# Placing side work behind sparse steps in the instruction order of a two-branch encoder kernel

## The chip, the cores and the metric

The kernel runs on one core of one Trainium2 chip. The metric is device time in microseconds (us) of one execution. The program is built by a tile framework: every instruction is traced in Python, the order of TensorE (PE) is kept as traced, and the order of the other engines (VectorE = DVE, ScalarE = ACT, GpSimd = POOL, and SyncE = SP, which issues nearly all DMAs) is chosen by a scheduler when the program is built, from its own estimate of when each instruction becomes ready. Among ready instructions the one traced first goes first. Once built, each engine's order is fixed.

## What is computed

Two sequences (1 x 1024 and 1 x 2048 tokens of width 1024) go through one encoder layer, each with the same 16 meta tokens ahead of it:

```
xn   = rmsnorm(h, g_pre);  proj = xn @ w_in + b_in          # 1024 -> 6672 columns
ya   = neighbourhood_attention(q, k, v) * silu(z)  @ w_a     # 8 heads of 64, 8 x 16 windows
yb   = mlstm_both_directions(conv(qk), v, gates) * silu(z) @ w_b   # 4 heads of 128
y    = (sigmoid(ga) * ya + sigmoid(gb) * yb) @ w_out
out  = h + rmsnorm(y, g_post)                                # meta tokens dropped
```

All of it is float32. The kernel reaches that by splitting every operand of a large product into a rounded high part and a low remainder and adding three products.

## The kernel before, in words

**Two streams on one TensorE.** `run` (L2070) interleaves two generators. `dense` does the projections and the output products; each of its yields stands for about 1.4 us of matmuls. `sparse` does, in the order of `STEPS`, the mLSTM of the short sequence, its attention, the mLSTM of the long sequence and its attention. Each of its yields ends a *sparse step* and gives a weight; `run` then advances `dense` until it has issued as much. So the traced order is: the instructions of one sparse step, then a dense chunk or two, then the next sparse step. Within the mLSTM a step holds, for example, `conv_c` (L1608 to L1612: the query q is finished and split), and the next but few hold `scores` (L1658), the matmul that reads q. Within the attention a unit's scores (L1210), exponential (L1225), scaling (L1235), transposes and their split (L1244, L1249) and output product (L1257) lie in steps that follow each other.

**Groups of dense work.** `PLAN` lists groups (sequence, first token of 1024, columns). The first is the short sequence's mLSTM columns, the second its attention columns, the third the first 1024 tokens of the long sequence with both kinds, the fourth the next 1024 tokens. A group (`group`, L1011) goes through jobs of four feature-major columns, each for two halves of 512 tokens, and token-major units. After each column a half is *evacuated* from PSUM (`fm_evac`: L682, L688 to L694 and a store).

**x's build.** `build_half` (L466) makes one half of the normalised input: it loads four token tiles (`tokens`, L398), squares them on ACT (L355), computes reciprocal roots on DVE (`rsqrt8`, L161 to L166), makes diagonals (L367, L369), spreads them over rows with a matmul (L375), loads the transposed input (`xt`, L405), scales it on DVE (L523), and splits it on ACT (L530) and DVE (L531). For the long sequence this happens four times. The tiles all come from four buffers called `xr`. The build is a generator; `spread` (L881) advances it a little at every dense yield: 12/15 of a piece per yield while the first part runs beside the last job of the group before (up to "scaled"), 22/15 otherwise.

**Side work.** Products of gate and attention columns are done later with Strassen-Winograd's seven products instead of eight. Their sums are made beforehand: `wprep` (L563) makes the sums of eight pairs of weight columns (raw tile `pr`, split to `po`: L567, L580, L589), 13 pieces a pair; `tprep` (L624) makes those of x (L627, L659, stores L663), 36 pieces for the short sequence; `nprep` (L597) those of six more pairs. `beside` (L545) is called once per dense yield and counts a turn; a piece of a side runs in every turn that its step divides. At the start of the first attention what is left of the weight sum is drained, in the last job of the second group what is left of x's sum.

**What holds a piece back.** `behind` (L189) puts every instruction traced inside it, by an ordering edge without a semaphore, behind the last marked instruction of its own engine. `mark` (L182) marks, for DVE, ACT and SP, the last instruction from a given position on:

```
for x in self.nc.cur_bb.bb.instructions[start:]:
    if x.engine in (DVE, Activation, SP):
        self.marks[x.engine] = x
```

Before the change only evacuations (`fm_evac`, `tm_unit`) mark. Pieces of the sides, the stores of kept x and the loads of the sums (`tload`, L909) are traced under `behind`; pieces of x's build are not.

Of the kernel before, what the change touches and what calls it, by code (L numbers as in the profile page):

```python
# [57 lines left out]
def _weight_units():  # L58

    return ([("i", x, P) for x in FM_COLS] + [("t", *c, a) for c in TM_COLS for a in range(2)]  # L60
            + [("m", f, P) for f in range(KT)] + [("o", c, a) for c in range(4) for a in range(2)])
# [76 lines left out]
class K:  # L138
# [327 lines left out]
    def build_half(self, s, t0, res):  # L466

        nc, wp = self.nc, self.wp
        if (s, t0) in self.xkept:
            assert not self.xput  # L470
            yield
            yield "scaled"
            x = []
            for name, part in zip(("xh", "xl"), self.xkept[s, t0]):
                x.append(wp.tile([P, KT, HALF], F32R, name=name, bufs=2))
                for k in range(0, KT, 4):
                    nc.sync.dma_start(x[-1][:, k:k + 4, :512].bitcast(F32), part[:, k:k + 4, :])
                yield
            res.append(tuple(x))
            return  # L480
        if s == 0:
            xts = self.xnext
            self.xnext = None
            while self.rwait:
                yield "wait"
            self.early = False
            yield "scaled"
            g = self.gpre
            p = self.psum("sm", [P, 512])
            nc.tensor.matmul(p[:, :KT], self.ident, g, start=True, stop=True)  # L490
            g = self.cp.tile([P, KT], F32, name="gx")
            nc.vector.tensor_copy(g, p[:, :KT])
            x, r = self.xparts(), []
            for e in range(4):
                self.xsplit(x, xts[e], e, 0, g)
                self.wflush(2)
                yield
            res.append(tuple(x))
            yield from self.rsum(self.toks, r)
            nc.vector.tensor_copy(self.rc[:, 4:8], r[0])  # L500
            dg = self.rdiag(r[0], self.toks[0][0])

            def rows():
                self.rrows(dg, self.rr[:, 1], "sm")
                self.xp.close()
                self.wside = self.wprep()
                self.sides.append([self.wside, 3])
            self.rwait[s, t0] = rows
        else:
            bp = self.bp  # L510
            toks, r = self.tokens(s, t0, range(4), bp, 4), []
            yield
            yield from self.rsum(toks, r)
            dg = self.rdiag(r[0], toks[3][0])
            xts = [self.xtload(s, t0, e, bp, 4) for e in range(3)]
            yield
            rr = bp.tile([P, 512], F32, name="rx", tag="thT", bufs=1)
            self.rrows(dg, rr, "pj")
            xts.append(self.xtload(s, t0, 3, bp, 4))
            yield  # L520
            for k in range(KT):
                v = xts[k // 2][:, k % 2]
                nc.vector.scalar_tensor_tensor(v, v, self.gpre[:, k:k + 1], rr, op0=ALU.mult, op1=ALU.mult)  # L523
                if k % 2:
                    yield
            yield "scaled"
            x = self.xparts()
            for e in range(4):
                h = x[0][:, 2 * e:2 * e + 2, :512]
                nc.scalar.activation(h, xts[e], AF.Copy)  # L530
                nc.vector.tensor_tensor(x[1][:, 2 * e:2 * e + 2, :512], xts[e], h.bitcast(F32), op=ALU.subtract)  # L531
                yield
            res.append(tuple(x))
            self.xkeep(s, t0, x)
# [28 lines left out]
    def wprep(self):  # L563

        nc = self.nc
        unit = {k: j for j, k in enumerate(_weight_units())}
        sub = lambda o, a, b: nc.vector.tensor_tensor(o, a, b, op=ALU.subtract)  # L567
        self.pq = ExitStack()
        pool = self.pq.enter_context(self.tc.tile_pool(name="pq", bufs=1, side="right", reuse_waits="tile"))
        for p in range(6, 14):  # L570
            if p == 12:
                [x for x in self.sides if x[0] is self.wside][0][1] = 6
            raw = pool.tile([P, 2, 2, 512], F32, name="pr", bufs=1)
            for f in range(2):
                nc.sync.dma_start(raw[:, f].rearrange("p a c -> p (a c)"), self.i["wu"][unit["i", PAIRS[p][f], P], :, :D])
            for _ in range(3):
                yield
            for f, ops in ((0, ("11", "12")), (1, ("21", "22")), (1, ("s3", "s1")), (0, ("s2", "s4"))):
                if ops[0] == "s3":
                    nc.vector.tensor_tensor(raw[:, 1, 1], raw[:, 1, 0], raw[:, 1, 1], op=ALU.add)  # L580
                    sub(raw[:, 1, 0], raw[:, 0, 0], raw[:, 1, 0])
                    yield
                if ops[0] == "s2":
                    sub(raw[:, 0, 0], raw[:, 1, 1], raw[:, 0, 0])
                    sub(raw[:, 0, 1], raw[:, 0, 1], raw[:, 0, 0])
                    yield
                o = pool.tile([P, 2, 2, 512], F32R, name="po", bufs=1)
                c = slice(p > 7 and ops[0] == "21", 2)
                nc.scalar.activation(o[:, c, 0], raw[:, f, c], AF.Copy)  # L589
                sub(o[:, c, 1], raw[:, f, c], o[:, c, 0].bitcast(F32))  # L590
                for q, op in list(enumerate(ops))[c]:
                    d = self.qd[p, op] = self.dp.tile([P, D], F32, name=f"q{p}{op}")
                    nc.sync.dma_start(d[:, :], o[:, q].rearrange("p a c -> p (a c)").bitcast(F32))
                yield
                yield
# [285 lines left out]
    def spread(self, gen, chunks, until=None):  # L881

        steps = 22 if until is None else 12

        def side(last=False):
            nonlocal acc, over
            acc += steps / chunks
            while not over and (acc >= 1.0 or last):
                acc -= 1.0
                x = next(gen, "end")  # L890
                over = x == "end" or (until is not None and x == until)
                if x == "wait":
                    break
        acc, over = 0.0, False
        return side
# [115 lines left out]
    def group(self, s, t0, meta, cols, reuse, nxt):  # L1011
# [4 lines left out]
        sw = (s, t0) in SW  # L1016
        if sw and not reuse:
            self.tside = chain(self.tprep(s, t0, 34 if s == 0 else 370 if t0 == 0 else 0), self.nprep() if t0 else ())
            self.sides.append([self.tside, 6 if s == 0 else 2 if t0 else 3])
        for j, (kind, c) in enumerate(jobs):  # L1020
            if kind == "tm":
                for cost in self.tm_unit(c[0], [(x,) + h for x, h in zip(self.xs, todo)], c[1]):
# [1047 lines left out]
    def run(self, ctx):  # L2070
        self.done = set()
        self.setup(ctx)
        dense, acc = self.dense(ctx), 0.0
        for w in self.sparse():
            if isinstance(w, tuple):
                while w not in self.done:
                    assert next(dense) is not True
                continue
            acc += w
            while acc > 0.0:  # L2080
                d = next(dense, None)
                if d is None or d is True:
                    acc = 0.0
                    break
                acc -= d
        for w in dense:
            assert w is not True

# [60 lines left out]
```

## Time and profile before

| | us |
|---|---|
| median of 3 runs | 2712.49 (2710.47 to 2716.36) |
| profiled execution | 2712.26 |
| its span in the trace | 2710.5 |
| PE busy | 2645.7 |
| DVE busy | 1937.3 |
| ACT busy | 1440.0 |
| mean granted clock of PE | 0.992 |

The profile gives each engine's busy time, groups of instructions by line, who waited for whom, the chain of work that ended last, and a timeline. L12 is line 12 of the kernel. "`A <- B`" behind a wait means that the engine of A stood idle until B was done. A granted clock below 1 means that TensorE was throttled in part of that stretch. Busy times of PE are modelled from matmuls that overlap; what counts here is PE's idle time.

### The profile page before, as it was taken

The numbers are of one execution on the slowest core, as the hardware profiler recorded it, in microseconds if no ns is written. First come the engines' busy times: TensorE is split into PE (matmuls) and PEld (weight loads), VectorE is DVE, ScalarE is ACT, GpSimd is POOL, SyncE is SP. The second block draws the span as 40 slices with busy tenths as digits, with TensorE's granted clock in tenths as the row PEclk, the third lists the DMA queues.
The fourth block names the chain that finished last, engine by engine and source line by source line (L and its number), as shares of the span: only waits on it lengthen the run. The fifth ranks groups of instructions, "written<-read, shape, count | busy, mean of one in ns | idle before, by whom it ended". The sixth has DMA issues, their size and how long they took to land.

```text
span 2710.5 us, 47460 instructions
## 1 busy us (share of the span) xinstructions
PE 2645.7 (98%) x15928; PEld 2334.1 (86%) x15928; DVE 1937.3 (71%) x5266; ACT 1440.0 (53%) x3388; POOL 16.9 (1%) x100
## 2 busy tenths in 40 slices
PE   9999998999998999999999999999999999999998
PEld 7998787889977899878888888888778998989888
DVE  5655787869847888536766767757368889897954
ACT  5323565665345655446655566556365656656521
POOL 0000000000000000000000000000000000000000
PEclk9999998999999999999999999999999999999999
DMA  9888898899896899798888998899899799998965
GB/s 363 342 321 317 295 340 297 306 338 314 280 322 210 307 329 310 239 311 266 265 283 293 368 311 263 281 323 378 259 300 298 246 311 274 293 294 280 329 230 203
DMA packets 411652, 805.75 MB, mean 297 GB/s; under 512 B 52016, under 2 KB 180992, under 8 KB 409104
## 3 DMA queue, kind: packets, MB, share of 16 engines
q1 hardware_dynamic: 410288, 800.04, 88.4%
q0 software_dynamic: 1120, 2.69, 0.4%
q8 instruction: 126, 2.06, 0.3%
q14 instruction: 118, 0.97, 0.1%
HBM read 548.96 MB, written 253.60 MB: 296 GB/s over the span
## 4 chain that ended last, share of the span: by engine, by line
PE 84%; DMA 6%; DVE 6%; ACT 2%; issue 1%; SPq 1%; DVEq 0%; ACTq 0%
PE pj L202 9%; PE pj L203 9%; PE pj L204 9%; PE pj L963 7%; PE pj L965 7%; PE pj L964 7%; PE pj L772 4%; PE pj L774 4%; PE pj L773 4%; PE pj L1908 3%; PE pj L1910 3%; PE pj L1909 3%; PE sm L1257 2%; PE tr L1242 2%; DMA xt<-xt 1%
## 5 line engine op out<-in xcount | busy, mean ns | idle before, releaser
L202 PE MATMUL pj<-xh,whi 128*128 128x512 f32 (+1 forms) x896 | 346.3, 387 | 2.0 <-ACT whi L303 2.0
L203 PE MATMUL pj<-xl,whi 128*128 128x512 f32 (+1 forms) x896 | 337.9, 377 | 0.1
L204 PE MATMUL pj<-xh,wlo 128*128 128x512 f32 (+1 forms) x896 | 337.6, 377 | 0.3 <-DVE wlo L304 0.3
L772 PE MATMUL pj<-whi,xh 128*128 128x256 f32 (+1 forms) x1152 | 330.1, 287 | 0.0
L773 PE MATMUL pj<-wlo,xh 128*128 128x256 f32 (+1 forms) x1152 | 325.1, 282 | 0.0
L774 PE MATMUL pj<-whi,xl 128*128 128x256 f32 (+1 forms) x1152 | 324.9, 282 | 0.0
L1908 PE MATMUL pj<-whi,mh 128*128 128x256 f32 x768 | 219.5, 286 | 0.7 <-DMA whi<-wh 0.7
L772 PEld LDWEIGHTS pj<-whi,xh 128*128 128x128 f32 x1152 | 217.4, 189 | 0.2
L773 PEld LDWEIGHTS pj<-wlo,xh 128*128 128x128 f32 x1152 | 217.4, 189 | 0.1
L774 PEld LDWEIGHTS pj<-whi,xl 128*128 128x128 f32 x1152 | 217.2, 189 | 0.0
L1910 PE MATMUL pj<-whi,mlo 128*128 128x256 f32 x768 | 216.4, 282 | 0.0
L1909 PE MATMUL pj<-wlo,mh 128*128 128x256 f32 x768 | 216.3, 282 | 0.0
L204 PEld LDWEIGHTS pj<-xh,wlo 128*128 128x128 f32 x896 | 170.4, 190 | 33.2 <-DVE wlo L304 0.5
L202 PEld LDWEIGHTS pj<-xh,whi 128*128 128x128 f32 x896 | 170.8, 191 | 30.4 <-ACT whi L303 2.9
L203 PEld LDWEIGHTS pj<-xl,whi 128*128 128x128 f32 x896 | 170.8, 191 | 26.7 <-issue 1.0
L202 PE MATMUL pj<-yh,whi 128*128 128x512 f32 x384 | 154.6, 402 | 0.0
L203 PE MATMUL pj<-yl,whi 128*128 128x512 f32 x384 | 151.2, 394 | 0.7 <-DVE yl L1810 0.7
L204 PE MATMUL pj<-yh,wlo 128*128 128x512 f32 x384 | 151.6, 395 | 0.0
L1244 ACT ACTIVATE pts<-tr 96x384 fp32r<-96x384 f32 (+2 forms) x192 | 103.2, 538 | 86.9 <-PE tr L1242 86.4
L1908 PEld LDWEIGHTS pj<-whi,mh 128*128 128x128 f32 x768 | 145.1, 189 | 1.7 <-DMA whi<-wh 0.9
L1909 PEld LDWEIGHTS pj<-wlo,mh 128*128 128x128 f32 x768 | 145.1, 189 | 0.8
L1910 PEld LDWEIGHTS pj<-whi,mlo 128*128 128x128 f32 x768 | 145.1, 189 | 0.0
(366 smaller groups left out, 6940.5 us busy)
## 6 DMA issues: line engine op xcount, KB each, us to landing
whi<-wh SPq DMA_DIRECT2D x136, 512.0 KB
wlo<-wl SPq DMA_DIRECT2D x136, 512.0 KB
whi<-q SPq DMA_DIRECT2D x62, 512.0 KB
wlo<-q SPq DMA_DIRECT2D x50, 512.0 KB
wraw<-wu SPq DMA_DIRECT2D x48, 512.0 KB
gt<-st SPq DMA_DIRECT2D x96, 256.0 KB
tg<-gt SPq DMA_DIRECT2D x96, 256.0 KB
wh<-whi SPq DMA_DIRECT2D x36, 512.0 KB
```

Of the source, the lines that this page charges most:

```text
L202: mm(out, ah, bh, start=start, stop=False)
L203: mm(out, ah, bl, start=False, stop=False)
L204: mm(out, al, bh, start=False, stop=stop)
L772: nc.tensor.matmul(o, xh, wh, start=k == 0, stop=False)
L773: nc.tensor.matmul(o, xh, wl, start=False, stop=False)
L774: nc.tensor.matmul(o, xl, wh, start=False, stop=k == KT - 1)
L963: mm(bank, w[:, 0, k], xh[:, k], start=fresh and k == 0, stop=False, skip_group_check=True)
L964: mm(bank, w[:, 0, k], xl[:, k], start=False, stop=False, skip_group_check=True)
L965: mm(bank, w[:, 1, k], xh[:, k], start=False, stop=k == 3, skip_group_check=True)
L1908: nc.tensor.matmul(o, mh[:, k, xs], wh, start=clear > 0 and k == 0, stop=False)
L1909: nc.tensor.matmul(o, mh[:, k, xs], wl, start=False, stop=False)
L1910: nc.tensor.matmul(o, ml[:, k, xs], wh, start=False, stop=clear < 2 and k == KT - 1)
```

## The change

There are four edits. `run` now takes the sparse generator step by step, notes where the instruction list stood, and marks the instructions of each sparse step, so that whatever is traced under `behind` next stands behind the last DVE, ACT and SP instruction of the latest sparse step or evacuation, whichever was traced later. `spread` advances x's build under `behind`. The weight sum runs in every fourth turn (before: every third, and from its seventh pair on every sixth). The short sequence's x sum runs in every fourth turn (before: every sixth).

```diff
@@ build_half
-                self.sides.append([self.wside, 3])
+                self.sides.append([self.wside, 4])
@@ wprep
         for p in range(6, 14):
-            if p == 12:
-                [x for x in self.sides if x[0] is self.wside][0][1] = 6
             raw = pool.tile([P, 2, 2, 512], F32, name="pr", bufs=1)
@@ spread
             while not over and (acc >= 1.0 or last):
                 acc -= 1.0
-                x = next(gen, "end")
+                with self.behind():
+                    x = next(gen, "end")
@@ group
-            self.sides.append([self.tside, 6 if s == 0 else 2 if t0 else 3])
+            self.sides.append([self.tside, 4 if s == 0 else 2 if t0 else 3])
@@ run
-        for w in self.sparse():
+        sparse, start = self.sparse(), 0
+        while (w := next(sparse, None)) is not None:
+            self.mark(start)
             if isinstance(w, tuple):
                 while w not in self.done:
                     assert next(dense) is not True
+                start = len(self.nc.cur_bb.bb.instructions)
                 continue
             acc += w
             while acc > 0.0:
...
                 acc -= d
+            start = len(self.nc.cur_bb.bb.instructions)
```

## The prediction

> **What bounds the kernel now.** I read the page's busy lines first, then the stage table (columns: stretch, length, busy time of PE, PEld, DVE, ACT, POOL with instruction counts, granted clock, DMA share, GB/s), then who PE waited for.
>
> ```profile
> span 2710.5 us, 47460 instructions
> PE 2645.7 (98%) x15928; PEld 2334.1 (86%) x15928; DVE 1937.3 (71%) x5266; ACT 1440.0 (53%) x3388; POOL 16.9 (1%) x100
> ```
>
> ```profile
> 0.00:250.00 250.00, 246.56 (x1619) 223.92 (x1620) 142.45 (x243) 102.18 (x153) 1.71 (x25) 1.00 0.90 335
> 250.00:420.00 170.00, 160.68 (x1037) 143.93 (x1036) 133.07 (x366) 92.64 (x215) 3.61 (x17) 0.97 0.90 319
> 420.00:600.00 180.00, 167.37 (x826) 138.64 (x825) 135.78 (x367) 107.34 (x258) 1.01 (x8) 0.96 0.91 313
> 600.00:745.00 145.00, 143.36 (x1206) 142.93 (x1204) 127.53 (x377) 67.69 (x170) 2.67 (x10) 1.00 0.90 302
> 745.00:960.00 215.00, 204.40 (x1108) 173.69 (x1107) 152.32 (x354) 122.02 (x244) 0.51 (x1) 0.98 0.85 278
> ```
>
> TensorE (PE) is the bound, and the edit changes no matmul. What can change is PE's idle time: 2710.5 − 2645.7 = 64.8 us, of which 9.3 + 12.6 + 1.6 + 10.6 = 34.1 us lie between 250 and 960 us, where x's build and the side work run beside sparse steps. Beyond 960 us only the loads of `tload` are touched. So the prize is about 34 us, and the clock that goes with it. PE's waits from 0 to 900 us (us in total, times, longest) say where it lies:
>
> ```profile
> PE sc L1658 <- DVE q L1612: 12.4, 2, 11.0
> PE tr L1789 <- DVE hb L1784: 3.2, 1, 3.2
> PE sc L1210 <- ACT prb L1225: 3.0, 1, 3.0
> PE sm L1257 <- DVE pts L1249: 2.8, 1, 2.8
> PE sm L1210 <- DVE yg L1272: 2.3, 1, 2.3
> PE sm L203 <- DVE vwl L1510: 2.0, 1, 2.0
> PE sm L1379 <- DVE g_eT L1381: 1.8, 1, 1.8
> ```
>
> Each is a sparse step's instruction that came late on DVE or ACT. The timelines up to the end of the longest, DVE, then ACT (start, length, what):
>
> ```profile
> 451.98 1.21 DVE L531 TENSOR_TENSOR xl<-xt,xh 128x1024 fp32r<-128x1024 f32 x1
> ...
> 453.38 3.49 DVE L531 TENSOR_TENSOR xl<-xt,xh 128x1024 fp32r<-128x1024 f32 x3
> ...
> 457.65 1.21 DVE L567 TENSOR_TENSOR po<-pr,po 128x1024 fp32r<-128x1024 f32 x1
> 458.79 0.41 DVE L1612 TENSOR_TENSOR q<-cv,q 128x256 fp32r<-128x256 f32 x1
> ```
> ```profile
> 448.37 0.42 ACT L1421 ACTIVATE th<-cv 128x256 f32<-128x256 f32 x1
> ...
> 449.20 3.88 ACT L530 ACTIVATE xh<-xt 128x1024 fp32r<-128x1024 f32 x4
> ...
> 454.12 1.05 ACT L589 ACTIVATE po<-pr 128x1024 fp32r<-128x1024 f32 x1
> 455.07 0.41 ACT L1611 ACTIVATE q<-cv 128x256 fp32r<-128x256 f32 x1
> ```
>
> In the program's order `conv_c` (L1608 to L1612) comes one sparse step ahead of the scores (L1658) at which PE stands. The four L530/L531 are issued only in the second half of the last job, after those scores. The scheduler let them overtake: 3.88 us on ACT and 1.21 + 3.49 us on DVE, and 1.05 and 1.21 us of a weight sum, ran ahead of L1611 and L1612. This is what the edit forbids.
>
> **The change part by part.** I count turns (calls of `beside`, one per dense yield). The first group has 24 half columns of 4 and 68 of its token-major units, 164; the second 132, to turn 296; the third 192, to 488. The rr matmul L375 is the eighth piece of a build, so at 0.8 a turn from turn 264 the first one of x_sample falls at turn 274, and at 1.47 a turn from 488 the last at 494:
>
> ```profile
> L375 PE MATMUL pj<-xr,ones x8: 590/591/592, 436.8 to 817.1; 128*128 128x512 f32 x8
> ```
>
> (817.1 − 436.8) / 220 = 1.73 us a turn.
>
> *Build behind the sparse step.* (a) At 448 us (459.2 − 11.0): L1421 ends at 448.8; with L530, L531 and the weight sum behind the scores, L1608 (no longer than its neighbours) and L1611 and L1612 (0.41 us each) and up to three evacuation pieces end near 452 instead of 459.2. Gain 7 us of 11.0 (bounds 0 and 11.0).
>
> ```profile
> 790.83 1.06 ACT L355 ACTIVATE xsq<-xr 128x1024 bf16<-128x1024 f32 x1 [0.88 <-DMA xr<-x_sample]
> ```
> ```profile
> 785.29 5.52 DMA xr<-x_sample
> ```
> ```profile
> 828.49 1.41 DVE L523 SCALAR_TENSOR_TENSOR xt<-xt,gpre,rx 128x512 f32<-128x512 f32 x2 [2.78 <-DMA xt<-xt]
> ```
>
> (b) PE's wait on prb: the square L355 waits for its load and stands ahead of the exponential L1225 that PE wants, though it is issued at turn 489 or 490, 4 turns (7 us) before the L375 at 817, so near 810. Pinned there it can't block: 2.5 of 3.0 us. (c) PE's waits on pts and yg: L531 and a sum (L627) run among the attention steps there: half of 2.8 + 2.3, so 2.5 us; the wait of 2.78 us for xt stays.
>
> *Step of x's sum, 6 to 4.* It starts at turn 36 and has 36 pieces: the last falls at turn 176 instead of 246. After turn 164 (about 250 us) 3 pieces are left instead of 14. Its DVE time from 250 to 420 us, and then that of the weight sum (what touches `pr`) in three stages:
>
> ```profile
> 250.00:420.00 170.00, 17.70 (x20) 0.97 0.90 319
> ```
> ```profile
> 250.00:420.00 170.00, 17.96 (x20) 9.64 (x10) 0.97 0.90 319
> 420.00:600.00 180.00, 8.30 (x9) 4.83 (x5) 0.96 0.91 313
> 600.00:745.00 145.00, 5.83 (x7) 2.72 (x3) 1.00 0.90 302
> ```
>
> So 11/14 × 17.7 = 13.9 us of DVE move ahead of 250 us, where DVE is 57% busy and PE idles 3.4 us, most of it the opening; I cost them at nothing there (bounds 0 and 8 us, since the slower weight sum takes 11 pieces, 5.8 us, out). They also free x's four `xr` buffers 70 turns earlier; the loads into these hold the squares on ACT now:
>
> ```profile
> 395.89 1.06 ACT L355 ACTIVATE xsq<-xr 128x1024 bf16<-128x1024 f32 x1 [4.04 <-DMA xr<-x_sample]
> ```
>
> (d) ACT's late work feeds PE's wait of 3.2 us for L1784: gain 2.5. (e) The waits on vwl and g_eT and what is left of L1658's (2.0 + 1.8 + 12.4 − 11.0 = 5.2 us) lie in that stage, where 8 of 34 weight pieces (4 us) go too and DVE falls from 78% to (133.1 − 17.9) / 170 = 68%: half, 2.6 (bounds 0 and 5.2).
>
> *Step of the weight sum, 3 and 6 to 4.* 104 pieces from turn 32 end at turn 444 instead of 416, just before the first mLSTM's end (about 453), so nothing is drained in a lump. Today 34 of them fall from turn 165 to 268, about the stage from 250 to 420 us: 17.96 / 34 = 0.53 us of DVE a piece. From 268 to 365 turns there are 8 more (4.2 us, DVE at 135.8 / 180 = 75%: 0.5 us charged), from 365 to 453 there are 11 more, 6 us where DVE is 127.5 / 145 = 88% busy: I charge 1.5 us (bounds 0 and 6).
>
> *What is queued.* A load that is pinned stands behind the sparse step's last SP issue, and its reader stands one or two pieces behind it. A square comes one piece after its load: 0.8 pieces a turn in a last job, 1.47 in a first, so 2.2 or 1.2 us later, and the load takes 5.5 us. ACT would hold 3.3 + 4.3 us for the two kinds, twice each: 15.2 us, with exponentials and evacuations behind it. Today's holds:
>
> ```profile
> ACT xsq L355 <- DMA xr<-x_sample: 36.5, 12, 21.2
> ```
>
> PE paid about 6.2 us (the 3.2 and the 3.0) for 36.5. At that rate 15.2 us cost 2.6; all of it would be 15.2. Nearer the former: 4 us. For `xt` (L405 to L523) I take today's holds as unchanged. The loads of `tload` and the stores of kept x go behind the same SP issues; several turns lie before their data is read, so 0 (bounds 0 and 3.0, PE's longest wait on ACT in the list). POOL is never marked.
>
> **Clock.** Stalls lower the granted clock:
>
> ```profile
> 450.00:500.00 50.00, 40.74 (x187) 33.66 (x187) 41.86 (x107) 36.34 (x85) 0.30 (x3) 0.86 0.92 326
> 800.00:850.00 50.00, 44.42 (x214) 35.83 (x213) 36.39 (x92) 27.31 (x57) 0.00 (x0) 0.97 0.59 179
> ```
>
> 0.14 × 50 = 7 us of full clock are missing around the longest stall, 1.5 us around 800. I take 3 us back (bounds 0 and 7). The Trainium skill (TensorE: Matmul & The Clock Gate, What's actually happening) has TensorE fall to half rate after an idle window of about 3.4 us. The stretch from 800 to 850 us, with the waits of 2.8 and 2.3 us, shows 0.97 all the same, so the measurement doesn't support that length as a floor; by the rule a stall cut from 11 to 4 us would still cost the clock, and the sum would lose those 3 us.
>
> **Sum.** −(7 + 2.5 + 2.5 + 2.5 + 2.6) − 3 + 0.5 + 1.5 + 4 = −14.1 us. The profiled execution took 2712.26 us, its span 2710.5, and the median shown is 2712.49: forecast **2698 us**.
>
> **The rivals.**
> *Slower: x's loads lose their lead.* One mechanism, in the four builds of x_sample: pinned loads land after their readers stand at the head of ACT and DVE. For it: L355 and L523 wait today already, and this load took longer than any gap here:
>
> ```profile
> 817.70 10.76 DMA xt<-xt
> ```
> ```profile
> DVE xt L523 <- DMA xt<-xt: 8.3, 3, 4.7
> ```
>
> L523 comes two pieces after its load, 4.3 or 2.4 us; holds are then up to 6.5 and 8.4 us, 29.8 us for four builds against 8.3 now. If PE pays the 15.2 us whole in place of 6.2 (9 more), half of the added 21.5, and 2 us for the fuller DVE, and only (a) with half the clock comes back (8.5), the time is 13 us longer: 2725 us. It decides from the point where PE pays two fifths of that (8.5 of 21.7). Against it: the row above holds a single wait of 21.2 us, and no wait of PE on ACT in the list is over 3.0 us. The Trainium skill (Perfetto Trace Analysis, Tensor Engine Instruction) calls ACT and DVE strict FIFO; the rows at 790.83 and 828.49 agree.
> *The wait only moves.* (a) shrinks, (c) and (e) come, with half the clock, but the displaced L530/L531 and the holds (9) and the fuller DVE (2) eat them: −7 − 2.5 − 2.6 − 1.5 + 9 + 2 = −2.6, 2710 us.
> *It doesn't do what it says.* The side work already stands behind evacuations; if the order written hardly differs, only the steps act, (d) and (e) less the weight sum's charges: 2712 − 5.1 + 2 = 2709 us. The overtaking rows speak against it.
>
> **How the numbers follow.** Forecast and its neighbours, −6 to −34 us (all waits (a) to (e) gone and the clock back: 27.5 + 7): 0.58, own range 2682 to 2706. The two unmoved cases: 0.09 and 0.06. Slower: 0.27. A measurement here can't tell less than 0.2% (5.4 us) from no change. The range runs from 2682 to 2728: below it lies 0.06 (nearly all terms at their bound), above it a little under half of the slower case, 0.12.
>
> **What would show it.** Right: around 448 us no L530/L531 between L1608 and L1612, and a wait at L1658 under 5 us; the last product of x's sum with `rr` (piece 29, turn 148) ahead of 250 us; the weight sum's end (turn 444) near 437 + 170 × 1.73 = 731 us; idle time from 250 to 960 us down to about 20 us. Wrong: L355 and L523 holding ACT and DVE for over 4 us each with PE waiting on L1225, L1249 or L1612 behind them; new waits from 600 to 745 us.

## The result and the profile after

The kernel after took 2739.0 us (median of 5 runs, 2735.37 to 2742.9), before took 2716.36 us beside it (5 runs, 3 of them those shown ahead of the prediction): ratio **1.0083, 95% interval 1.0058 to 1.0107**. The change makes the kernel 0.8% slower. The profiled execution took 2738.11 us.

The busy lines of after, then its stage table (columns as in the table of before):

```profile
span 2736.3 us, 47461 instructions
...
PE 2652.4 (97%) x15928; PEld 2337.9 (85%) x15928; DVE 1943.8 (71%) x5266; ACT 1443.9 (53%) x3388; POOL 17.3 (1%) x100
```
```profile
250.00:420.00 170.00, 167.44 (x1100) 150.69 (x1099) 128.17 (x361) 90.98 (x221) 3.81 (x16) 1.00 0.83 287
420.00:600.00 180.00, 157.69 (x748) 128.72 (x747) 131.19 (x356) 104.31 (x243) 1.12 (x9) 0.93 0.86 309
600.00:745.00 145.00, 142.83 (x1188) 142.39 (x1188) 128.65 (x369) 71.89 (x174) 2.68 (x10) 0.99 0.93 318
745.00:960.00 215.00, 189.39 (x988) 158.77 (x988) 143.82 (x335) 113.22 (x223) 0.52 (x1) 0.94 0.79 266
```

Length less PE's busy time is its idle time: 2.6, 22.3, 2.2 and 25.6 us. The first stage gained as forecast (9.3 before); the second and the fourth lost 9.7 and 15.0 us, and their granted clock fell from 0.96 and 0.98 to 0.93 and 0.94. Over the whole span PE's idle time rose by 19.1 us (83.9 against 64.8), and its busy time, for the same matmuls, by 6.7 us. PE's waits up to 960 us (us in total, times, longest) name one place:

```profile
PE pj L375 <- ACT xr L367: 41.9, 4, 16.4
PE sc L1657 <- DVE q L1611: 4.4, 1, 4.4
PE tr L1528 <- DVE kf L1492: 2.2, 1, 2.2
```

The old waits are nearly gone; 41.9 us stand at L375, the matmul that spreads the reciprocal roots over rows (the *rr matmul*), once in each of the four builds of x_sample. Before, it never waited. From 250 to 960 us PE idles 52.7 us in all, 34.1 before; without the 41.9 us it would be 10.8. The last build on PE, before and then after (start, length, what, idle time ahead):

```profile
816.65 1.02 PE L375 MATMUL pj<-xr,ones 128*128 128x512 f32 x2
817.11 0.79 PE L202 MATMUL pj<-xh,whi 128*128 128x512 f32 x1
```
```profile
842.36 2.07 PE L375 MATMUL pj<-xr,ones 128*128 128x512 f32 x2 [8.23 <-ACT xr L367]
843.45 1.41 PE L202 MATMUL pj<-xh,whi 128*128 128x512 f32 x1
```

The pair also took 2.07 instead of 1.02 us, and the matmul behind it 1.41 instead of 0.79: after the stall the clock is low. Why L367 is late shows best in build 3. SP's queue in after, then DVE and PE around it:

```profile
761.60 1.21 SPq L829 DMA_DIRECT2D nv<-stT  x2
762.86 0.62 SPq L1144 DMA_DIRECT2D gt<-rpb  x1
...
767.02 0.30 SPq L1168 DMA_DIRECT2D vr<-nv  x1
767.37 0.86 SPq L296 DMA_DIRECT2D wlo<-wl  x1
768.28 2.78 SPq L398 DMA_DIRECT2D xr<-x_sample  x4
```
```profile
756.79 0.42 DVE L788 TENSOR_TENSOR stT<-pj,bb 128x256 f32<-128x256 f32 x1 [2.41 <-PE pj L772]
783.91 0.17 DVE L358 TENSOR_SCALAR ss<-ss 128x4 f32<-128x4 f32 x1 [26.69 <-ACT xsq L355]
...
786.29 0.48 DVE L369 TENSOR_SCALAR xr<-ident,nwy 128x128 f32<-128x128 f32 x2
```
```profile
787.08 2.08 PE L375 MATMUL pj<-xr,ones 128*128 128x512 f32 x2 [16.44 <-ACT xr L367]
```

The token loads L398 stand behind the attention's loads (L1144 to L1168) and are issued at 768.28 us. Their four squares end at 783.9, the pinned L358, the first instruction of the roots, has held DVE for 26.7 us by then, and the diagonals come at 786.3, though PE has stood at L375 since 770.6 (787.08 − 16.44). In before the first load of this build was issued 17 us earlier:

```profile
751.49 0.92 SPq L398 DMA_DIRECT2D xr<-x_sample  x2
```
```profile
765.04 0.69 ACT L367 ACTIVATE xr<-ident,nwy 128x128 f32<-128x128 f32 x2 [1.90 <-DVE nwy L166]
...
767.04 1.02 PE L375 MATMUL pj<-xr,ones 128*128 128x512 f32 x2
```

So *lead*, the time from ACT's start on the diagonals (L367) to PE's start at L375, was 767.0 − 765.0 = 2 us in build 3 of before. Where PE waits, I count the wait as a lead below zero: −16.4 us in after. In build 1 of before it was 436.8 − 410.3 = 26 us (ACT, then PE), in after −8.5 us:

```profile
410.34 0.69 ACT L367 ACTIVATE xr<-ident,nwy 128x128 f32<-128x128 f32 x2 [3.48 <-DVE nwy L166]
```
```profile
436.77 1.02 PE L375 MATMUL pj<-xr,ones 128*128 128x512 f32 x2
```
```profile
432.50 2.07 PE L375 MATMUL pj<-xr,ones 128*128 128x512 f32 x2 [8.51 <-ACT xr L367]
```

Every trace holds the same 15,928 matmul records, so the start of the n-th one can be subtracted from that of the n-th one of before: negative means ahead. This running difference, in us, at a time of before (single profiled executions, and executions of one kernel differ by several us in all; the rr matmul's own place moves a little in some kernels, the rest is in the same order):

```
at us of before:   250    420    480    560    700    780    960   1200   end
after              0.0  -12.1   -9.3    0.7    3.8   22.1   18.5   23.6  25.9
```

So the edit does gain 12 us up to 420 us, as the forecast wanted, and then pays at L375: twice from 420 to 500 us and twice from 770 to 850 us, each time with the low clock on top.

### The profile page after: what moved, and what is told of

Its sections match the earlier page's. It is cut to its first block, busy times and chain, and to the rows that moved or that the text cites. A ratio compares the mean times of both kernels' runs of the same rounds, so it can differ in the third digit from the quotient of the medians.

```text
span 2736.3 us, 47461 instructions
## 1 busy us (share of the span) xinstructions
PE 2652.4 (97%) x15928; PEld 2337.9 (85%) x15928; DVE 1943.8 (71%) x5266; ACT 1443.9 (53%) x3388; POOL 17.3 (1%) x100
## 4 chain that ended last, share of the span: by engine, by line
PE 58%; DMA 6%; DVE 4%; ACT 2%; issue 1%; SPq 0%; DVEq 0%; ACTq 0%
PE pj L962 7%; PE pj L964 7%; PE pj L963 7%; PE pj L202 5%; PE pj L203 5%; PE pj L204 5%; PE pj L1907 3%; PE pj L1908 3%; PE pj L1909 3%; PE sm L1256 2%; PE tr L1241 2%; PE pj L770 1%; PE pj L772 1%; DMA stk<-nq 1%; PE pj L771 1%
```

## The experiments

**Which part costs?** First the parts, each against before or after.

*e1_build_free*: after, without the pin in `spread`.
```diff
-                with self.behind():
-                    x = next(gen, "end")
+                x = next(gen, "end")
```


> The changed kernel, but x's build is not traced behind the marks (sparse marks and both steps of four stay). Theory (starved rows matmul): the pinned build reaches the matmul that spreads rr (L375) too late, and PE, whose order is fixed, stands there 41.9 us; without the pin that wait falls to under 3 us and the time to 2695 to 2712 us. Rival (the marks and steps cost elsewhere, L375 only shows it): some other wait takes over and the time stays above 2728 us.

*e5_steps_only*: before with both sums in steps of four. *e9_xsum_only* and *e10_wsum_only*: one of the two each.
```diff
-                self.sides.append([self.wside, 3])
+                self.sides.append([self.wside, 4])
...
-            if p == 12:
-                [x for x in self.sides if x[0] is self.wside][0][1] = 6
...
-            self.sides.append([self.tside, 6 if s == 0 else 2 if t0 else 3])
+            self.sides.append([self.tside, 4 if s == 0 else 2 if t0 else 3])
```


> The kernel before with both sums in steps of four and nothing else. As charged in the forecast (waits d and e less the fuller DVE): about 3 us faster than before, 2709 us against 2712. Rival (the later weight sum costs more than the earlier x sum gives): 5 to 10 us slower than before. Under the theory of the starved matmul no wait over 3 us in total appears at L375.

> The kernel before with x's sum alone in steps of four. If the earlier x sum frees the xr buffers and lets the free build run ahead into the mLSTM's first steps, the 10 us of wait at the transpose of kf (L1528 of the changed kernel) that the run with both steps shows come back here, the wait at the scores of 448 us is about 5 us, and at L375 there is none: 2708 to 2718 us. If the waits at kf come from the weight sum, they are absent here and the kernel is 5 to 10 us faster than before.

> The kernel before with the weight sum alone in steps of four. If the later weight sum crowds the last turns before the third build, the wait of 8 to 13 us at L375 near 770 us, seen in all runs with steps of four, shows here too, and the kernel is 5 to 12 us slower than before. If the x sum is what makes it, L375 waits under 2 us here and the time stays within 5 us of before.

*e6_marks_only*: before plus the marks behind sparse steps (the edit of `run` alone). *e7_old_steps*: after with the old steps, so e6 plus the pin in `spread`. *e8_pin_evac*: before plus that pin alone, marks of evacuations only.
```diff
-                x = next(gen, "end")
+                with self.behind():
+                    x = next(gen, "end")
```


> The kernel before with sparse steps marked as well, so that the side work alone stands behind them: build free, old steps. Theory (pin and steps cost, marks don't): within 6 us of before, PE's wait at L375 under 3 us in all and at the scores of 448 us still over 8 us, since the build is what overtakes there. Rival (the marks hold the side work up): slower by over 8 us, with new waits from 600 to 960 us.

> The changed kernel with the old steps (3, then 6, and 6): marks and pinned build alone. Theory (the pin starves the rows matmul): waits at L375 in all four builds, 25 to 40 us in all, and 12 to 25 us slower than before. Rival (the steps of four make the builds late): under 10 us of wait at L375, and no slower than 5 us.

> The kernel before with one thing added: what a call of spread emits of x's build is put behind marked instructions too, but the marks are the old ones, of evacuations alone; sums with their old steps, no marks behind the sparse steps. Theory A (any pin behind an already queued instruction starves the rr matmul, because the piece of work is held until the marked instruction's place comes up on its engine): L375 waits 25 to 40 us in all, in all four builds, and the time is 2726 to 2740 us. Theory B (it needs the marks of the sparse steps, which come later in the engines' orders than the evacuations'): L375 waits under 8 us in all, builds 1, 2 and 4 under 2 each, and the time is within 0.3% of before, 2706 to 2722 us.

Measured (ratio to before with its 95% interval; L375's wait and its longest, and the longest other wait of PE up to 960 us, in us):

| kernel | pin of build | sparse marks | steps of 4 | median us | ratio | L375 | other |
|---|---|---|---|---|---|---|---|
| after | yes | yes | both | 2739.0 | 1.0083 (1.0058 to 1.0107) | 41.9, 16.4 | 4.4 |
| e1 | no | yes | both | 2715.89 | 1.0010 (0.9997 to 1.0024) | 13.1, 13.1 | 5.2 |
| e5 | no | no | both | 2717.23 | 1.0019 (1.0007 to 1.0032) | 7.8, 7.8 | 5.1 |
| e9 | no | no | x sum | 2716.98 | 1.0021 (1.0004 to 1.0037) | 0 | 5.1 |
| e10 | no | no | weight sum | 2723.21 | 1.0033 (1.0016 to 1.0050) | 6.4, 6.4 | 7.2 |
| e6 | no | yes | none | 2722.0 | 1.0030 (1.0017 to 1.0043) | 13.4, 13.4 | 5.2 |
| e7 | yes | yes | none | 2735.81 | 1.0082 (1.0059 to 1.0106) | 33.9, 10.9 | 3.7 |
| e8 | yes | no | none | 2742.84 | 1.0111 (1.0090 to 1.0131) | 42.7, 12.1 | 3.9 |

PE's waits in e8, the pin alone, and in e1, all but the pin:

```profile
PE pj L375 <- ACT xr L367: 42.7, 4, 12.1
```
```profile
PE pj L375 <- ACT xr L367: 13.1, 1, 13.1
PE tr L1527 <- DVE kf L1491: 10.1, 2, 5.2
PE sc L1656 <- DVE nwt L164: 5.0, 1, 5.0
```

**The pin is the cost**: it alone gives 1.0111, and taking it from after leaves 1.0010. (`spread` also advances the loads of the output products, L1804, from 2016 us on; e8 pins these too and loses nothing behind 960 us, as the running difference below shows.) Whether the marks are those of sparse steps hardly matters for it (e8 against e7). Without the pin only build 3 waits, and only when side work there runs later or is marked. No part is faster than before by itself. Several expectations were missed: e1 was to wait under 3 us at L375 and to stay below 2712 us, and waited 13.1; e5 and e6 were to show no wait over 3 us there, and e6 to stay within 6 us of before, where it was 8.3 above; e5 came out 3.5 us slower than before, which neither of its readings had. e7, e8, e9 and e10 went the way of the reading that blames the pin or the step concerned, though e8's wait and time lie a little above their ranges and e10's wait below its own.

Two readings of mine fell here. The 11.0-us wait at the scores (L1658 in before) shrank to 5.0 us in e5 as well, which pins nothing, and no single wait there is over 7.2 us in e1, e6, e9 or e10: in every other kernel here that stall is shorter, pinned or not, so it belongs to one order and is not something that only the pin can take away (e6's expectation has that miss). And the x sum's step, freely built, opens a new wait in e5, and in e9, which changes that step alone (9.3 us in two). DVE, ACT and PE of e5 at 290 us, where the freed `xr` buffers let the build run far ahead:

```profile
290.21 0.16 DVE L358 TENSOR_SCALAR ss<-ss 128x4 f32<-128x4 f32 x1
...
292.59 0.48 DVE L369 TENSOR_SCALAR xr<-ident,nwy 128x128 f32<-128x128 f32 x2
...
296.52 1.94 DVE L1508 SCALAR_TENSOR_TENSOR vwl<-va,g_wT,vwh 128x130 fp32r<-128x130 f32 x7
298.37 0.42 DVE L1491 SCALAR_TENSOR_TENSOR kf<-th,cv 128x256 f32<-128x256 f32 x1
```
```profile
292.65 0.69 ACT L367 ACTIVATE xr<-ident,nwy 128x128 f32<-128x128 f32 x2 [1.62 <-DVE nwy L166]
...
294.20 0.49 ACT L1414 ACTIVATE cv<-raw,cw 128x256 f32<-128x256 f32 x1
```
```profile
298.85 0.69 PE L1527 MATMUL tr<-ident,kf 128*128 128x128 f32 x2 [5.11 <-DVE kf L1491]
```

Roots and diagonals, whose reader comes 140 us later, run ahead of `kf`, for which PE stands. On ACT the diagonals wait 1.62 us for the roots, and L1414, with which the chain of `kf` begins, comes behind them; how much of the 5.11 us is theirs is not shown, since DVE also does seven `vwl` ahead of `kf`. In after this wait is 2.2 us. So the pin does remove an overtaking, and pays for it at L375.

**Which piece of the build?** *e2_loads_free*: after, but the four token loads of each build are not pinned. *e3_pin_late*: after, but a build is pinned only from its rr matmul on.
```diff
-                with self.behind():
+                with self.behind() if self.late else ExitStack():
```
(`self.late` is set false where `spread` begins a build of x_sample, and true after the first piece in e2, after L375 in e3.)

> The changed kernel, but the first piece of each long-sequence build, which holds nothing but the four token loads, is traced outside the marks; squares, roots and diagonals stay pinned. If the late loads on SP starve the matmul, PE's wait at L375 falls from 41.9 us to under 10 us and the time to 2695 to 2712 us. If the pinned squares and roots on ACT and DVE do it by themselves, the wait stays over 25 us and the time above 2722 us.

> The changed kernel, but each long-sequence build is pinned only from the matmul at L375 on (its scaling L523 and splits L530 and L531, and the last load of xt). Theory (starved rows matmul): the wait at L375 is gone and the gain at the scores stays: 2688 to 2702 us, below both kernels. Rival (pinned splits cost as well, by pushing what follows): 2705 us or more, no better than with a free build.

e2 took 2735.31 us, 1.0091 (1.0077 to 1.0105): the rr matmul (L376 there) still waited 34.8 us, 4.1, 8.7, 17.9 and 4.0 in the four builds. An early load helps builds 1 and 4 by half and the others not at all, since squares, roots and diagonals stay where they are. e3 took 2728.4 us, 1.0065 (1.0049 to 1.0081): builds 1, 2 and 4 no longer wait, but build 3 does, and both the overtaking at `kf` and a wait on the pinned split itself stand in the list (the rr matmul is L376 there):

```profile
PE pj L376 <- ACT xr L368: 18.2, 1, 18.2
PE tr L1532 <- DVE kf L1496: 10.1, 2, 5.2
...
PE pj L204 <- DVE xl L533: 4.0, 1, 4.0
```

I had put e3 near the forecast; it is a miss, and a warning against picking pieces of a chain.

**Is it lead?** If the chain of loads, squares, roots and diagonals is merely late for a reader at a fixed place, moving the reader back, or the chain forward, must cure it. *e4_rows_later*: after, with the cut between two jobs ahead of the rr matmul, so that in builds 1 and 3 it comes some six turns later.
```diff
             xts = [self.xtload(s, t0, e, bp, 4) for e in range(3)]
-            yield
+            yield "scaled"
             rr = bp.tile([P, 512], F32, name="rx", tag="thT", bufs=1)
...
-            yield "scaled"
             x = self.xparts()
```


> The kernel after (marks, steps of four and pinned builds), but the yield that the written order calls scaled stands ahead of the rr matmul of a half-build and not behind the square roots' rows: in the two builds whose chain is cut there (builds 1 and 3) the rr matmul L375 is then written some six turns, 10 to 12 us, later on the in-order TensorE, while loads, squares, roots and diagonals keep their pinned places. Nothing else changes. Theory (the pinned chain loads, squares, roots, diagonals is late for a reader whose place is fixed): the waits of L375 in builds 1 and 3 (8.7 and 16.6 us in the kernel after) fall by about 10 us each, to 0 to 1 and 5 to 8; those of builds 2 and 4 (8.9 and 8.4) stay within 1.5 us of that; the sum of L375's wait falls from 41.9 to 22 to 28 us and the time to 2719 to 2732 us. Rival (the wait is not one of lead: the chain is triggered by the same event that frees PE, so that it moves with L375): the sum stays at 38 to 43 us and the time at 2734 to 2742.

*e11_early_start*: e4, and loads, squares, roots and diagonals of the second half are handed out one job earlier.
```diff
-                        side = self.spread(nb, 15)
+                        self.half2 = self.build_half(nxt[0], nxt[1] + 512, nres)
+                        side = self.spread(chain(nb, self.half2), 15, "scaled", 22)
```
(The first job of the next group goes on with `self.half2`, and `spread` takes its pieces per 15 yields as a fourth argument.)

> The kernel of e4_rows_later, with the second half of each of the two spread builds started ahead: its token loads, squares, roots and diagonals are handed out in the job before, behind the first half's pieces, and only its rr matmul and what follows stay in the job where they were. All of it stays pinned, with marks behind the sparse steps and steps of four. Theory (lead is all that the pinned chain lacks): the waits of L375 fall to under 1.5 us each in builds 1, 2 and 4 and to at most 8 in build 3, the other waits stay at about 42 us, and the time is 2694 to 2714 us. Rival (the pinned pieces cost by holding ACT, DVE or SP themselves, wherever they are): the idle time of L375 turns up at other waits of PE of the same stages and the time is 2724 to 2740 us.

*e12_more_lead*: e11 with empty pieces ahead of each rr matmul, because in e11 it had become the first piece of its job and so had moved forward too; the last job now hands out 28 pieces to 15 yields.
```diff
-                    gen, self.half2 = self.half2 or self.build_half(*todo[1][:2], self.xs), None
+                    gen = chain([None] * 7, self.half2) if self.half2 else self.build_half(*todo[1][:2], self.xs)
+                    self.half2 = None
...
-                        side = self.spread(chain(nb, self.half2), 15, "scaled", 22)
+                        side = self.spread(chain([None] * 6, nb, self.half2), 15, "scaled", 28)
```


> The kernel of e11_early_start, with seven empty pieces ahead of the second half's rr matmul and six ahead of the first half's (28 pieces to 15 units there): the rr matmuls of builds 2 and 4 are written again at exactly the place that they have in the kernel after, those of builds 1 and 3 some twenty PE instructions (about 5 us) later than in e11, while loads, squares, roots and diagonals stay where e11 has them. In e11, L376 (the rr matmul there) waited 8.7, 4.9 and 10.3 us in builds 2, 3 and 4, because with the first pieces handed out earlier the rr matmul had itself become the first piece of its job. Theory (lead between the chain and the rr matmul is all that the pinned build lacks): L376 waits under 6 us in all, PE's other waits stay near 42 us, and the time is 2690 to 2706 us, below before. Rival (held ACT and SP time has to be paid somewhere on the way to the half's first matmul): the rr matmul's wait moves to L203/L204 on xl or xh, or to kd, pts and yg waits, 15 us or more of them, and the time stays at 2710 to 2725 us.

The waits of the rr matmul (L376 in the last two), in the order e4, e11, e12:

```profile
PE pj L375 <- ACT xr L367: 25.1, 3, 10.6
```
```profile
PE pj L376 <- ACT xr L368: 23.4, 3, 10.0
```
```profile
PE pj L376 <- ACT xr L368: 6.0, 2, 4.5
```

and the row of build 1 in e4, at full speed and with no idle time ahead of it:

```profile
440.31 1.07 PE L375 MATMUL pj<-xr,ones 128*128 128x512 f32 x2
```

e4: 2722.15 us, 1.0031 (1.0018 to 1.0045), as its theory had it: build 1 waits no more, build 3 went from 16.4 to 4.6 us, and builds 2 and 4 waited 10.6 and 9.9. e11: 2715.11 us, 1.0000 (0.9986 to 1.0014), 1 us above its theory's range, and its L376 still waited 23.4 us: the chains of builds 2 and 4 came earlier, and so did their readers. e12: 2712.2 us, 0.9994 (0.9981 to 1.0008): with the second halves' rr matmul back in its place of after and the chain ahead of it, 35.9 of the 41.9 us are gone, and so is the loss of time. **The cause is lead**, shown from both ends.

But e12's expected time, below 2706, was missed, and the time lies in its rival's range. The rival's mechanism showed in part: PE's idle time from 250 to 960 us without that of the rr matmul is 19.9 us in e12 against 10.8 in after, so some 9 us turn up elsewhere (of the waits that the rival names, `yg` has 3.0 us, `kd` 2.9 and `pts` 1.1, not 15 or more). The running difference against before (as above) tells where:

```
at us of before:   250    420    480    560    700    780    960   1200   end
e1                 0.6    1.0   -5.9   -7.1   -6.0   11.2   -0.9    5.0   5.8
e5                 0.7    0.0   -7.0   -6.3   -2.4   10.3    0.2    0.8   3.6
e6                 1.0   -4.0   -2.6   -3.9   -4.3   11.3    2.3   11.6  13.5
e7                 0.9   -4.4    0.1    8.1    7.8   21.5   17.6   19.8  21.1
e8                -0.2   -2.0    4.2   16.9   16.9   30.4   30.3   30.3  31.0
e11                0.6  -12.2  -23.3  -12.0  -10.7   -2.7    0.9    4.5   3.8
e12                1.5   -8.9  -21.9  -12.8  -10.8   -3.2   -8.8    2.0   1.9
e13               -0.2   -7.1  -19.6   -9.9   -6.3    1.7   -3.9   -1.5   2.6
e14                0.0   -6.6  -13.6   -3.3   -3.2   -1.7   -7.1   -2.3   2.6
```

(e13 and e14 follow below.) e12 is 8.8 us ahead at 960 us and 2.0 behind at 1200. Its longest waits there, then that of before:

```profile
PE sm L1259 <- ACT prb L1227: 4.8, 3, 3.9
```
```profile
PE sm L1257 <- ACT prb L1225: 1.3, 1, 1.3
```

**Where does the rest go?** *e13_lead_evac*: e12 without the marks behind sparse steps. *e14_lead_xsum*: e13 with the old steps of the weight sum (both edits are those of `run` and `wprep`, taken back).

> The kernel of e12_more_lead (pinned build, earlier start, rr matmul where the kernel after has it) with the marks of evacuations alone, none behind the sparse steps; both sums still in steps of four. Between the 960th and the 1200th microsecond of before, the PE matmul with the same number comes 5 to 11 us later, against before, in the runs with marks behind sparse steps (e3, e4, e6, e12 and after itself), and 0 to 1 us in e5, e8 and e9, which have none. Theory (the marks behind sparse steps put the weight sum's and the attention side's pieces ahead of ACT's exponentials there): that loss goes to under 3 us, the wait of the p.v matmul on prb falls from 10.3 to under 6 us, and the time is 2698 to 2709 us, below before. Rival (the loss there comes with the early build or the weight sum's step, or without the sparse marks the rr matmul's waits return, 12.1 us at their longest in e8): the time is 2710 to 2722 us.

> The kernel of e13_lead_evac with the weight sum's steps of before (3, then 6), so that of the change only the pinned build and the x sum in steps of four are left, with the lead added. Theory (the weight sum in steps of four costs by itself: 0.33% alone, with 11 to 15 us lost between 760 and 780 us of before by the rr matmul of build 3 and again late in the span): build 3's wait of L376 falls to under 2 us and the time is 3 to 8 us below that of e13, 2692 to 2706 us. Rival (with lead for the rr matmul the weight sum's step no longer matters): within 3 us of e13.

e13: 2712.17 us beside 2715.03 of before, 0.9987 (0.9975 to 0.9999). e14: 2712.12 us, 0.9986 (0.9975 to 0.9997). From 960 to 1200 us e13 lost 2.4 us and e14 4.8 where e12 lost 10.8, and the wait on `prb` there is 1.4 us again:

```profile
PE sm L1259 <- ACT prb L1227: 1.4, 1, 1.4
```

Four pairs of kernels differ in the marks behind sparse steps alone, and in each the one with them loses more in that stretch: e6 9.3 us and before nothing, e1 5.9 and e5 0.6, e12 10.8 and e13 2.4, e7 2.2 and e8 0. The sizes differ too much for one price: e11, with marks, loses 3.6 us and e14, without, 4.8. Nor is `prb` the whole of it, since after and e11 wait only 1.1 and 0.9 us on it there. What the marks certainly hold in that stretch is `nprep` (L601 before, L599 in after), side work that DVE does there:

```profile
L601 DVE TENSOR_TENSOR xr<-xr 128x512 f32<-128x512 f32 (+1 forms) x32 | 28.0, 882 | 0.6 <-DMA xr<-wu 0.5
```
```profile
L599 DVE TENSOR_TENSOR xr<-xr 128x512 f32<-128x512 f32 (+1 forms) x36 | 30.6, 859 | 8.6 <-issue 5.0 <-DMA xr<-wu 1.9 <-DMA gg<-stT 1.5
```

DVE stood idle ahead of it for 8.6 us in after against 0.6; whether PE pays for that is not shown. But e13's time did not fall by that: without these marks it comes to 960 us with a smaller lead, L376 waiting 8.7 us and `kf` 5.0. e14's expected 3 to 8 us below e13 did not come; its rival, no difference, did. Both end just under before, by about 3 us, which is below the 0.2% that I had taken as the least that a measurement here can tell. What stays open: which marked pieces cost PE time between 960 and 1200 us, and why the 4 to 7 us by which e13 and e14 lead at 960 us are gone at the end of their traces. Part of the latter is chance: the traced executions of e13 and e14 took some 2.5 us more than their medians, that of before (2712.26 us) up to 4 us less than the medians of before in these comparisons.

## Why the prediction was wrong

The forecast was 2698 us (2682 to 2728), faster; 2739.0 us came out. Step by step:

- *What bounds the kernel*: PE's idle time is the right quantity. After has 2736.3 − 2652.4 = 83.9 us against 64.8, and from 250 to 960 us 52.7 instead of the 20 forecast. That beyond 960 us only the loads of `tload` are touched was wrong: `nprep` runs there behind the marks, and each of the four pairs above loses time there.
- *(a) the scores, gain 7 of 11.0 us*: size right, reason wrong. The wait is 4.4 us, and no L530 or L531 stands any more between L1607 and L1611 (L1608 and L1612 of before), as the row set for it asked; but two L531 (2.35 us from 457.96 us) now stand straight ahead of L1607, inside that wait, and e5 gives 5.0 us with no pin.
- *(b) to (e)*: of these waits `yg`, `prb` and `g_eT` are left up to 960 us, with 0.5, 0.4 and 0.3 us. The size was right, even cautious, up to 960 us: there e12, with the waits of the rr matmul nearly gone, leads before by 8.8 us, and at the end it does not.
- *x's sum*: the last product with `rr` came at 226.2 us (ahead of 250, as forecast), at no cost while pinned. That it also lets a free build overtake (e5) was not seen.
- *Weight sum*: its last split came at 729.2 us (731 forecast). Charged 2 us; alone it costs 0.33%, with 6.4 us of it at L375 of build 3.
- ***What is queued*, the step that failed.** It priced pinned loads by what stands behind a waiting square on ACT: 15.2 us held, 4 us paid. ACT's holds were sized well (16.6 us), and PE's other waits on ACT up to 960 us are 1.0 us or less each:

```profile
ACT xsq L355 <- DMA xr<-x_sample: 16.6, 6, 7.6
```

  The price lies at the end of the chain. The step followed each pinned instruction to its *next* reader and never to the one on PE, the engine whose order is fixed: L375 was used in the text only as a clock for counting turns. The hold on DVE at L358 was not in it either (10.7 us, the longest 9.1, in the same stretch of before):

```profile
DVE ss L358 <- ACT xsq L355: 31.3, 4, 26.7
```

  Measured in place of the 4 us: 41.9 us at L375, in four builds.
- *The clock*: 3 us of gain expected, a loss came: PE's busy time rose by 6.7 us, of which the half-speed pairs at L375 are about 1 us each.
- *The slower rival* had the loads' lost lead as its mechanism and 2725 us as its price; it was nearest. It too looked for the cost at L355 and L523, so its "wrong" sign showed by half: L355 held ACT for up to 7.6 us, but behind that PE waited at L375 and not on L1225, L1249 or L1612. *The wait only moves* named the right kind of outcome at the wrong place.

The Trainium skill (Perfetto Trace Analysis, Tensor Engine Instruction) calls ACT and DVE strict FIFO, and the 26.69 us that DVE stood behind L358 agree. Its clock rule (TensorE: Matmul & The Clock Gate, What's actually happening), half rate after some 3.4 us of idling, agrees with the pair of 2.07 us after a stall of 8.23 us; e4's pair of 1.07 us had no stall ahead of it. The length is no floor here, as the last section shows.

## What to carry to other kernels

When an edit holds work back, follow its chain to the end, to the reader on the engine whose order is fixed, and compare the lead the chain has now with the lead it will have: here the chains of loads, squares, roots and diagonals lost 18 us of lead in build 3 and 35 in build 1, and the forecast had priced only their first reader. A scheduler's overtaking that looks like a stall's cause may be what pays for another reader's lead; undoing it is only free together with an earlier start (e12). And a single long wait in one schedule is weak evidence for a gain, when a schedule changed elsewhere (e5) dissolves it as well.

## What the runs showed of the hardware

TensorE's granted clock was 0.72 from 765 to 795 us of after, the stretch with the longest stall, and the first matmuls after a stall ran at half speed:

```profile
765.00:795.00 30.00, 13.56 (x50) 9.97 (x49) 7.56 (x22) 10.05 (x18) 0.00 (x0) 0.72 0.88 262
```

I had not expected that a stall of 8 us takes the clock down for the matmuls behind it in each of the four builds alike, so that a stall costs more than its length: 1.05 us at the pair and 0.62 at the matmul behind it in the last build. Shorter stalls can do it too, and with a delay. In e13 a stall of 2.31 us ends at 781.66 us; the next matmuls of 128x512 still take 0.39 to 0.40 us, but those from 783.26 us on 0.63, and the pair of build 3 behind them 1.91 with no stall directly ahead of it:

```profile
781.66 0.40 PE L1212 MATMUL sc<-kd,stk 128*128 128x288 f32 x1 [2.31 <-ACT kd L1187]
...
782.76 0.40 PE L203 MATMUL pj<-xh,whi 128*128 128x512 f32 x1
...
783.26 0.63 PE L205 MATMUL pj<-xh,wlo 128*128 128x512 f32 x1
783.68 1.91 PE L376 MATMUL pj<-xr,ones 128*128 128x512 f32 x2
```
